# A hybrid mLSTM, HGRN and attention trunk: two-tile VectorE operations in scalar-tensor-tensor form, weight sums on VectorE outside HGRN, a recurrence whose two directions share their operations, and other places for some weight matmuls

## The chip, the cores and the metric

The kernel runs on one core of a Trainium2 chip. The metric is the device time of one execution in microseconds (us); what is compared is the median of several executions. TensorE is PE in the profile (its weight loads are PEld), VectorE is DVE, ScalarE is ACT, GpSimd is POOL and SyncE is SP. SP issues all the DMAs of the kernel. Within an engine, instructions run in the order of its queue: one that waits holds up all behind it.

## The reference

A trunk of two layers over 1024 tokens of width 1024, in fp32. Each layer normalises its input, multiplies it with one wide weight matrix, and feeds the columns of the product to three groups, whose outputs are gated, joined and projected back:

```python
proj = einsum("bsd,de->bse", rms_norm(x, norm_g[l]), w_in[l])
(xm, om, zm, hq, hff, hfb, hi, hz, aq, ak, av, az) = split(proj)
# mLSTM, 4 heads of 192, both directions, in chunks:
#   C, n are decayed and take in k v^T and k;  h = num / max(|den|, exp(-m_t))
hm  = sigmoid(om) * mlstm_bidirectional(mq, mk, mv, gates)
y_m = (head_rms_norm(hm) + m_skip[l] * xc) * silu(zm)      # xc = silu(conv(xm))
# HGRN, 6 heads of 128, both directions: S_t = diag(f_t) S_{t-1} + (1 - f_t) i_t^T, o_t = S_t^T q_t
f   = lb + (1 - lb) * sigmoid(hff or hfb)
y_h = head_rms_norm(hgrn2_bidirectional(hq, f_fwd, f_bwd, hi)) * silu(hz)
# differential attention, 4 heads: (softmax(Q1 K1^T) - lam softmax(Q2 K2^T)) V, partly rotated q and k
y_a = head_rms_norm(differential_attention(...)) * silu(az)
x   = x + einsum("bse,ed->bsd", concat(y_m, y_h, y_a), w_out[l])
```

## The kernel before

**The projection as a stream.** The product with `w_in` is cut into 32 units of four 512-wide weight quadrants each. The last 29 (`unit`, L197) are computed with seven products of 12 matmuls in place of eight, Strassen's way: a unit loads four quadrants (wraw), makes sums of them (ws, the four lines L213, L215, L229 and L236, on POOL), splits quadrants and sums into a rounded part (whi, ACT) and a rest (wlo, POOL), both L153 to L161, and adds the PSUM results to outputs c (DVE L221, L241, L247; ACT L252), which go to DRAM. `unit` is a generator that yields after every matmul and `fill(n)` (L467) draws n steps of it, so that weight matmuls (named ua, ub, ud) are strewn among the work of the stages as filler. `STEPS` is 84. The weight buffers are few: five of wraw, five each of whi and wlo, three of ws.

**The stages of a layer**, with their stretch of the span in us for the first layer (the second begins at 1590 and runs alike):

1. 0 to 294: norm, transposes, the first units, the convolution and gates of mLSTM. The convolution's last step is L612, its taps are L603 to L607.
2. 294 to 511: mLSTM (L733 to L829). First 420 steps of the stream, then four heads. In a head's recurrence, 8 chunks i for each of two directions d: products num and st on PE, n on ACT and DVE (L803, L804), the state C updated by two instructions (L815, L816: 128 and 64 rows of 193 columns), the denominator by three instructions of one column (L820 to L822), and n/den put or added into hsum (L825, L827). The two buffers of the tag m8 are shared by q (copied by ACT, L756) and hsum.
3. 511 to 972: HGRN, six heads in `hgrn(hd)` (L838 to L1019), a generator in three pieces, so that a head's end and the next head's start interleave. A head transposes v (hvt), turns the gate into ks and T (ACT L861, DVE L862 and L864), adds kd (L867), multiplies qp (L868, L869), multiplies kd with q (dg), then runs seven levels: each does matmuls lv between ks and qp and then multiplies both, in place, with decays T (DVE L938 and L939, one instruction over both directions) and halves T (L943). Then come kst, sb, sf, ho; squares of ho (ACT L1003, tile jk); `rstd` (L414 to L422, sums hss, tiles rs and hr); ho scaled (ACT L1009); its transposes (hyT), and the product hyo (L1017), which a DMA stores.
4. 972 to 1211: called md here. The rest of mLSTM: so is loaded (its DMA from pr_om), goes through ACT (L1069) and is transposed by PE (soT, L109), then gates hp (L1078); the convolution xcp is scaled on POOL (L1100); `rotate` turns the rotary columns (L1050 to L1052). 672 steps of the stream are placed behind marks, and then all that are left.
5. 1198 to 1482: attention (L1120 to L1215); 1277 to 1589: the output projection (op).

**What sets the order.** In mLSTM and HGRN `seq["on"]` is true, and every matmul and transpose is issued after the one before it in the program (`in_order`, L107): there the order on PE is that of the text, and the counts in `M_FILL` and `H_FILL` (L79, L80) say how many weight steps stand at each point. `H_FILL["tail"]` steps stand ahead of the first HGRN head of a layer. Elsewhere, and on all other engines everywhere, a list scheduler sets the order from estimated times. Buffers of the HGRN pool are shared by md's tiles and come free when the last head's instructions and its store are done.

Of the kernel before, what the change touches and what calls it, by code (L numbers as in the profile page):

```python
# [9 lines left out]
F32 = mybir.dt.float32  # L10
# [3 lines left out]
AF = mybir.ActivationFunctionType  # L14
# [65 lines left out]
H_FILL = {"hvt": 0, "ty": 32, "dg": 10, 0: 14, 1: 14, 2: 10, 3: 10, 4: 10, 5: 8, 6: 14, "kst": 10, "sb": 8, "ho": 10, "tail": 28}  # L80
# [15 lines left out]
def trunk(ctx, tc, x_in, positions, w_in, w_out, pvec, rvec, out, dbg=None):  # L96
# [20 lines left out]
    def tr(*a, **k):  # L117
        return in_order(nc.tensor.transpose, *a, **k)

# [47 lines left out]

    def w_tmp():
        cnt["n"] += 1
        return wp.tile([P, 512], F32, tag="ws", name=f"ws{cnt['n']}", bufs=3)  # L170
# [26 lines left out]
    def unit(l, u, B, dst):  # L197
# [15 lines left out]
        nc.gpsimd.tensor_tensor(s1, a21, a22, op=ALU.add)  # L213
        s2 = w_tmp()
        nc.gpsimd.tensor_tensor(s2, s1, a11, op=ALU.subtract)  # L215
# [13 lines left out]
        nc.gpsimd.tensor_tensor(s3, a11, a21, op=ALU.subtract)  # L229
# [6 lines left out]
        nc.gpsimd.tensor_tensor(s2, a12, s2, op=ALU.subtract)  # L236
# [169 lines left out]
    def rstd(ss, r, width):  # L406
# [12 lines left out]
        for _ in range(3):  # L419
            nc.vector.tensor_tensor(a, r, r, op=ALU.mult)  # L420
# [14 lines left out]
    for l in range(DEPTH):  # L435
# [50 lines left out]
        for half in range(2):  # L486
# [26 lines left out]
            else:  # L513
# [10 lines left out]
                for k in range(4):  # L524
# [9 lines left out]
                    tt = nc.vector.tensor_tensor  # L534
# [17 lines left out]
        if True:  # L552
# [47 lines left out]
            def post_xm(j, xm):  # L600
# [11 lines left out]
                nc.vector.tensor_mul(xc, xc, th)  # L612
# [37 lines left out]
        flr = m1.tile([P, 2, NT, 4], F32, name="flr")  # L650
        dec = m1.tile([P, 2, NT, 4], F32, name="dec")
        with tc.tile_pool(name=f"mb{l}", bufs=1) as mB:
# [27 lines left out]
            for d in range(2):  # L680
# [14 lines left out]
                nc.vector.tensor_sub(ir, ir, br)  # L695
# [27 lines left out]
            nc.vector.tensor_add(flr, b_tok, m_tok)  # L723
# [5 lines left out]
        with tc.tile_pool(name=f"mc{l}", bufs=1) as mp:  # L729
            for hd in range(MH):  # L730
# [60 lines left out]
                for i in range(NT):  # L791
                    for d in range(2):
# [5 lines left out]
                        n = mp.tile([P, MD + 1], F32, name=f"n{l}{hd}{d}{c}", tag="n", bufs=2)  # L798
# [8 lines left out]
                        if i < NT - 1:  # L807
# [3 lines left out]
                            pc2 = pc[r0:r0 + 64, 256:256 + MD + 1]  # L811
# [3 lines left out]
                            nc.vector.scalar_tensor_tensor(C[:, 0], C[:, 0], dc, pc[:, :MD + 1], op0=ALU.mult, op1=ALU.add)  # L815
                            nc.vector.scalar_tensor_tensor(C[r0:r0 + 64, 1], C[r0:r0 + 64, 1], dc[r0:r0 + 64], pc2,  # L816
                                                           op0=ALU.mult, op1=ALU.add)
                        fill(M_FILL[3])
                        den = mp.tile([P, 1], F32, name=f"den{l}{hd}{d}{c}", tag="den", bufs=4)
                        nc.vector.scalar_tensor_tensor(den, n[:, MD:], -1.0, n[:, MD:], op0=ALU.mult, op1=ALU.max)  # L820
                        nc.vector.tensor_tensor(den, den, flr[:, d, c, hd:hd + 1], op=ALU.max)
                        nc.vector.reciprocal(den, den)  # L822
                        if c not in seen:
                            seen.add(c)
                            nc.vector.tensor_scalar_mul(hsum[:, c], n[:, :MD], den)  # L825
                        else:
                            nc.vector.scalar_tensor_tensor(hsum[:, c], n[:, :MD], den, hsum[:, c], op0=ALU.mult, op1=ALU.add)  # L827
# [10 lines left out]
        def hgrn(hd):  # L838
# [19 lines left out]
            for d in range(2):  # L858
# [5 lines left out]
                nc.vector.tensor_scalar(th, th, lb_a1[:, l, d, hd:hd + 1], lb_a2[:, l, d, hd:hd + 1],  # L864
                                        op0=ALU.mult, op1=ALU.add)
            kd = slab(f"kd{hd}", "ha")
            nc.vector.tensor_tensor(kd, ks[:, 0], ks[:, 1], op=ALU.add)  # L867
            nc.vector.tensor_tensor(qp[:, 0], T0[:, 0], q, op=ALU.mult)  # L868
            nc.vector.tensor_tensor(qp[:, 1], T0[:, 1], q, op=ALU.mult)  # L869
# [18 lines left out]
            for lv in range(7):  # L888
# [44 lines left out]
                el = [[2 * hs, nb], [hs + S, 2], [1, hs]]  # L933
                tq = raw(T, 1, [[2, nb], [W - 1, 2], [0, hs]])
                tk = raw(T, W + 1, [[2, nb], [-W - 1, 2], [0, hs]])
                qv = raw(qp, 0, el)
# [410 lines left out]
```

## Time and profile before

| what | value |
| --- | --- |
| median of 3 runs | 3160.61 us (3159.49 to 3163.45) |
| the profiled execution's own time | 3164.39 us |
| its span | 3162.7 us |
| granted clock of PE, mean | 0.945 |
| busy: PE / DVE / ACT / POOL | 87% / 66% / 42% / 40% |

The profile is of one execution. A line of a group names the source line, the engine, the operation, out<-in by the program's names, the shapes, the count, then busy us and the mean ns of one, then the idle time of the engine ahead of them and what ended most of it. A line of waits names an engine's line, what it waited for, and us in total, times and the longest. A line of windows gives a stretch of the span, its length, the busy us (and instructions) of PE, PEld, DVE, ACT and POOL, PE's granted clock (1 is full), the DMA engines' busy share and GB/s. L109 is the matmul helper where the order is free, L111 where it is pinned.

### The profile page before, as it was taken

What the parts mean: (1) busy time and instruction counts of PE and PEld (TensorE: products, weight loads), DVE (VectorE), ACT (ScalarE), POOL (GpSimd) and SP (SyncE); (2) the same over time, 40 slices, a digit from 0 to 9 for tenths busy, and PEclk for the clock granted to TensorE, in tenths of its full rate; (3) what the DMA queues carried; (4) which work ended last, traced back from release to release, by engine and by line L of the source; (5) the groups of instructions that cost most, each with busy time, mean ns of one, the idle gap of its engine ahead of it and who ended that gap; (6) DMA issues with size and microseconds to landing.
All of it is one profiled execution on the core that took longest, in us unless ns stands there. A gap on an engine that the chain in (4) does not pass through costs nothing. (4 is left out here: it accounts for less than half of the span.)

```text
span 3162.7 us, 45081 instructions
## 1 busy us (share of the span) xinstructions
PE 2736.3 (87%) x16428; PEld 2242.7 (71%) x16428; DVE 2100.3 (66%) x3792; ACT 1320.4 (42%) x2732; POOL 1251.0 (40%) x881
## 2 busy tenths in 40 slices
PE   6888998888887998998979999978887889989987
PEld 4766877666665776887858787856666667768875
DVE  7775757777674526997587545767777644389964
ACT  5333443333433435654153344434433344365533
POOL 4255232454444771010243643234544457501012
PEclk9899999999998998999989999999999889989998
DMA  3333332222224654520223333232222256552221
GB/s 106 112 128 114 108 133 97 94 91 89 89 77 146 209 169 117 169 81 28 87 72 116 123 124 124 94 115 90 94 90 91 68 203 200 155 154 84 71 67 74
DMA packets 186526, 352.00 MB, mean 111 GB/s; under 512 B 17968, under 2 KB 67632, under 8 KB 186304
## 3 DMA queue, kind: packets, MB, share of 16 engines
q1 hardware_dynamic: 186304, 349.12, 33.4%
q8 instruction: 129, 2.11, 0.3%
q14 instruction: 93, 0.76, 0.1%
HBM read 234.69 MB, written 114.36 MB: 110 GB/s over the span
## 5 line engine op out<-in xcount | busy, mean ns | idle before, releaser
L161 POOL TENSOR_TENSOR wlo<-wraw,whi 128x512 fp32r<-128x512 f32 x262 | 404.7, 1554 | 1138.1 <-ACT whi L160 954.2
L161 POOL TENSOR_TENSOR wlo<-ws,whi 128x512 fp32r<-128x512 f32 x232 | 364.5, 1572 | 425.1 <-ACT whi L160 401.8
L109 PE MATMUL op<-whi,yb 128*128 128x512 f32 x1024 | 342.1, 402 | 1.5 <-DVE ayo L1163 0.7
L160 ACT ACTIVATE whi<-ws 128x512 fp32r<-128x512 f32 x232 | 145.8, 629 | 403.1 <-PE ua L109 161.3
L160 ACT ACTIVATE whi<-wraw 128x512 fp32r<-128x512 f32 x262 | 163.6, 627 | 313.5 <-issue 104.2
L109 PE MATMUL ua<-Bt,whi 128*128 128x512 f32 x698 | 231.4, 413 | 25.1 <-DVE c L241 24.2
L111 PE MATMUL ua<-Bt,whi 128*128 128x512 f32 x694 | 243.9, 424 | 4.6 <-DVE c L241 4.5
L1253 DVE TENSOR_TENSOR xo<-op,xo 128x512 f32<-128x512 f32 x256 | 173.9, 686 | 90.6 <-PE op L109 89.8
L109 PEld LDWEIGHTS op<-whi,yb 128*128 128x128 f32 x1024 | 193.9, 190 | 46.4 <-DVE xo L1253 1.8
L109 PE MATMUL op<-wlo,yb 128*128 128x512 f32 x512 | 203.0, 396 | 0.0
L1187 ACT ACTIVATE e<-S,mx 128x1024 f32<-128x1024 f32 x128 | 142.3, 1113 | 109.8 <-DVE mx L1184 45.3
L109 PEld LDWEIGHTS ua<-Bt,whi 128*128 128x128 f32 x698 | 135.2, 197 | 60.9 <-DVE c L241 27.0
L1183 DVE TENSOR_REDUCE mx<-S 128x1 f32<-128x1024 f32 x128 | 155.5, 1217 | 18.2 <-PE S L109 17.6
L111 PEld LDWEIGHTS ua<-Bt,whi 128*128 128x128 f32 x694 | 133.5, 196 | 35.1 <-DVE c L241 8.2
L109 PE MATMUL po<-av,wT 128*128 128x128 f32 x1024 | 139.8, 283 | 16.2 <-ACT wT L1203 9.7
L109 PEld LDWEIGHTS po<-av,wT 128*128 128x128 f32 x1024 | 131.4, 197 | 26.8 <-ACT wT L1203 13.1
L938 DVE TENSOR_TENSOR ks<-ks,T 128x1024 f32<-128x1024 f32 x84 | 141.5, 1684 | 11.0 <-ACT kt L894 10.5
L111 PE MATMUL ua<-Bt,wlo 128*128 128x512 f32 x348 | 147.4, 424 | 0.0
L939 DVE TENSOR_TENSOR qp<-qp,T 128x1024 f32<-128x1024 f32 x84 | 142.0, 1691 | 4.1 <-PE lv L111 4.1
L109 PE MATMUL ua<-Bt,wlo 128*128 128x512 f32 x348 | 141.8, 408 | 0.0
L109 PE MATMUL S<-qkh 128*128 128x512 f32 x256 | 111.9, 437 | 23.9 <-ACT e L1187 23.6
L894 ACT ACTIVATE kt<-ks 128x1024 f32<-128x1024 f32 x60 | 71.2, 1186 | 140.4 <-DVE ks L938 52.5
(437 smaller groups left out, 7011.9 us busy)
## 6 DMA issues: line engine op xcount, KB each, us to landing
wraw<-w_in SPq DMA_DIRECT2D x256, 256.0 KB
wraw<-yT SPq DMA_DIRECT2D x64, 256.0 KB
wraw<-w_out SPq DMA_DIRECT2D x64, 256.0 KB
xac<-xcd SPq DMA_DIRECT2D x16, 512.0 KB
W<-mu SPq DMA_DIRECT2D x32, 256.0 KB
xcd<-xc SPq DMA_DIRECT2D x12, 512.0 KB
xct<-tka SPq DMA_DIRECT2D x12, 512.0 KB
vd<-tkv SPq DMA_DIRECT2D x12, 512.0 KB
```

Of the source, the lines that this page charges most:

```text
L109: return fn(*a, **k)
L111: seq["last"] = fn(*a, **k)
L160: nc.scalar.activation(hi, src, AF.Copy)
L161: (lo_eng or nc.gpsimd).tensor_tensor(lo, src, hi.bitcast(F32), op=ALU.subtract)
L894: nc.scalar.activation(raw(kt, 0, [[2 * hs, nb], [hs, 2], [1, hs]]), raw(ks, 0, [[2 * hs, nb], [hs + S, 2], [1, hs]]), AF.Copy)
L938: nc.vector.tensor_tensor(kv, kv, tk, op=ALU.mult)
L939: nc.vector.tensor_tensor(qv, qv, tq, op=ALU.mult)
L1183: nc.vector.tensor_reduce(mx, ps, axis=AX.X, op=ALU.max)
L1187: nc.scalar.activation(e, ps, AF.Exp, scale=QK ** -0.5, bias=mx, accum_out=ls_)
L1253: nc.vector.tensor_tensor(xv, ps, xv, op=ALU.add)
```

## The change

Six edits, none of which changes what is computed:

1. `dtt(out, a, b, op)` issues (a * 1.0) op b as scalar_tensor_tensor, and takes the place of tensor_tensor for almost all DVE instructions with two SBUF tiles: in `rstd`, the convolution, HGRN (kd, qp, ks, T), rotate, attention's splits and the output projection's. In HGRN's levels, the instruction over both directions becomes one for each direction from level 1 on (128x512 each); level 0 stays one.
2. `wsum` puts the four weight sums of a unit on POOL while `sums["pool"]` is set, which it is from before the first HGRN head of a layer until after the last, and on DVE otherwise: 22 units of the 58 stay on POOL, 36 go to DVE, by the orders of the two kernels.
3. In the mLSTM recurrence the n of both directions lies in one tile nn. The three denominator instructions run once for both (two columns; flr is laid out for it), the C update is one instruction over both halves (386 columns), and the first hsum of a chunk is put by ACT; the second is added by DVE as before.
4. The second gate instruction of HGRN (L864) goes from DVE to ACT, as Identity with scale and bias.
5. The scaling of xcp (L1100) goes from POOL to ACT.
6. `H_FILL["tail"]` is 60 in place of 28, and 48 steps of the stream stand between the last HGRN head of a layer and md. md's own fixed counts stay, so 80 fewer steps are left for its end.

Where instructions move, in three places. First PE at the end of the first layer's HGRN stage: the last head's transposes (hyT), and md's first (soT). Before, no weight step lies between them:

```order
L111 MATMUL ud_22_8183<-Bt_0_350,whi_8159 128x512 x2
L111 MATMUL hyT_8193<-ident,ho_8121 128x128 x4
L111 MATMUL hyT_8199<-ident,ho_8121 128x128 x4
L109 MATMUL soT_8216<-ident,so_8213 128x128 x4
L109 MATMUL soT_8222<-ident,so_8213 128x128 x4
L109 MATMUL ud_22_8183<-Bt_0_350,wlo_8160 128x512
```

In the changed kernel the 48 steps begin and end so:

```order
L111 MATMUL hyT_8099<-ident,ho_8027 128x128 x4
L111 MATMUL hyT_8105<-ident,ho_8027 128x128 x4
L111 MATMUL ua_22_7794<-Bt_0_353,whi_8075 128x512
L111 MATMUL ua_22_7794<-Bt_0_353,wlo_8076 128x512
L111 MATMUL ua_22_7794<-Bt_0_353,whi_8075 128x512 x2
```

```order
L111 MATMUL ua_23_8139<-Bt_0_351,wlo_8159 128x512
L111 MATMUL ud_23_8202<-Bt_0_350,whi_8178 128x512 x2
L111 MATMUL ud_23_8202<-Bt_0_350,wlo_8179 128x512
L109 MATMUL soT_8216<-ident,so_8213 128x128 x4
L109 MATMUL soT_8222<-ident,so_8213 128x128 x4
```

The end of unit 22 and more than the first half of unit 23 now lie between hyT and soT. (At the start of HGRN it is alike: 32 more steps ahead of the first hvt.)

Second, DVE where the third HGRN head of the first layer begins and the second ends. Before (L862, L864 and kd, qp are the new head's; rs begins the old head's rstd):

```order
L862 TENSOR_SCALAR ks_5636<-T_02_5634,nlb_a_114,lb_a_112 128x1024 x2
L864 TENSOR_SCALAR T_02_5634<-T_02_5634,lb_a_112,lb_a_113 128x1024 x2
L867 TENSOR_TENSOR kd_5757<-ks_5636 128x1024
L869 TENSOR_TENSOR qp_5635<-T_02_5634,hq_5637 128x1024
L868 TENSOR_TENSOR qp_5635<-T_02_5634,hq_5637 128x1024
L416 TENSOR_SCALAR rs_5657<-hss_5567 128x8
```

In the changed kernel (L877 is L862 of before, L121 is `dtt`, L252 is L241, L427 is L416):

```order
L877 TENSOR_SCALAR ks_5504<-T_02_5502,nlb_a_114,lb_a_112 128x1024 x2
L121 SCALAR_TENSOR_TENSOR kd_5612<-ks_5504 128x1024
L121 SCALAR_TENSOR_TENSOR qp_5503<-T_02_5502,hq_5505 128x1024 x2
L252 TENSOR_TENSOR c_15_5574<-ua_15_5312,p_15_5555 128x512
L427 TENSOR_SCALAR rs_5525<-hss_5445 128x8
```

The two T instructions are gone from this queue, and an evacuation c of unit 15 has come to stand ahead of rs.

Third, DVE at the end of the first layer's HGRN stage. Before, the end of the last head's rstd, its two products hyo, and md's first hp:

```order
L421 SCALAR_TENSOR_TENSOR rs_8122<-rs_8122 128x8
L422 SCALAR_TENSOR_TENSOR hr_8064<-rs_8122,hr_8064 128x8
L1017 SCALAR_TENSOR_TENSOR hyo_8192<-hyT_8193,hgs,hz_8065 128x512
L1017 SCALAR_TENSOR_TENSOR hyo_8192<-hyT_8199,hgs,hz_8065 128x512
L1078 SCALAR_TENSOR_TENSOR hp_8210<-soT_8216,hp_8210 128x4x128
```

In the changed kernel (L432, L433 are L421, L422 of before, L1032 is L1017, L232 is L221, L1096 is L1078):

```order
L432 SCALAR_TENSOR_TENSOR rs_8028<-rs_8028 128x8
L433 SCALAR_TENSOR_TENSOR hr_7971<-rs_8028,hr_7971 128x8
L121 SCALAR_TENSOR_TENSOR ws_8469<-wraw_8442,wraw_8444 128x512
L1032 SCALAR_TENSOR_TENSOR hyo_8098<-hyT_8099,hgs,hz_7972 128x512
L1032 SCALAR_TENSOR_TENSOR hyo_8098<-hyT_8105,hgs,hz_7972 128x512
L121 SCALAR_TENSOR_TENSOR ws_8471<-ws_8469,wraw_8438 128x512
L121 SCALAR_TENSOR_TENSOR ws_8513<-wraw_8438,wraw_8442 128x512
L232 TENSOR_TENSOR c_23_8175<-ub_23_8162,p_23_8152 128x512
L1096 SCALAR_TENSOR_TENSOR hp_8210<-soT_8216,hp_8210 128x4x128
```

The three sums of unit 24 now stand in DVE's queue, the first ahead of hyo, and each waits there for its weight loads (wraw).

The diff, cut to its core (`-` before, `+` after):

```diff
-H_FILL = {"hvt": 0, "ty": 32, "dg": 10, 0: 14, 1: 14, 2: 10, 3: 10, 4: 10, 5: 8, 6: 14, "kst": 10, "sb": 8, "ho": 10, "tail": 28}
+H_FILL = {"hvt": 0, "ty": 32, "dg": 10, 0: 14, 1: 14, 2: 10, 3: 10, 4: 10, 5: 8, 6: 14, "kst": 10, "sb": 8, "ho": 10, "tail": 60}
...
+    def dtt(out_, a, b, op):
+        nc.vector.scalar_tensor_tensor(out_, a, 1.0, b, op0=ALU.mult, op1=op)
...
+    sums = {"pool": False}
+
+    def wsum(o, a, b, op):
+        if sums["pool"]:
+            nc.gpsimd.tensor_tensor(o, a, b, op=op)
+        else:
+            dtt(o, a, b, op)
...
-        nc.gpsimd.tensor_tensor(s1, a21, a22, op=ALU.add)
+        wsum(s1, a21, a22, ALU.add)
...
-                nc.vector.tensor_mul(xc, xc, th)
+                dtt(xc, xc, th, ALU.mult)
...
                 for i in range(NT):
+                    nn = mp.tile([P, 2, MD + 1], F32, name=f"n{l}{hd}{i}", tag="n", bufs=2)
                     for d in range(2):
...
-                        n = mp.tile([P, MD + 1], F32, name=f"n{l}{hd}{d}{c}", tag="n", bufs=2)
+                        n = nn[:, d]
...
-                            nc.vector.scalar_tensor_tensor(C[:, 0], C[:, 0], dc, pc[:, :MD + 1], op0=ALU.mult, op1=ALU.add)
-                            nc.vector.scalar_tensor_tensor(C[r0:r0 + 64, 1], C[r0:r0 + 64, 1], dc[r0:r0 + 64], pc2,
-                                                           op0=ALU.mult, op1=ALU.add)
+                            pc2 = pc.rearrange("p (b n) -> p b n", b=2)[:, :, :MD + 1]
+                            nc.vector.scalar_tensor_tensor(C, C, dc, pc2, op0=ALU.mult, op1=ALU.add)
                         fill(M_FILL[3])
...
-                        nc.vector.tensor_tensor(den, den, flr[:, d, c, hd:hd + 1], op=ALU.max)
+                    nc.vector.tensor_tensor(den, den, flr[:, i, hd], op=ALU.max)
...
-                            nc.vector.tensor_scalar_mul(hsum[:, c], n[:, :MD], den)
+                            nc.scalar.activation(hsum[:, c], nn[:, d, :MD], AF.Copy, scale=den[:, d:d + 1])
...
-                nc.vector.tensor_scalar(th, th, lb_a1[:, l, d, hd:hd + 1], lb_a2[:, l, d, hd:hd + 1],
-                                        op0=ALU.mult, op1=ALU.add)
+                nc.scalar.activation(th, th, AF.Identity, scale=lb_a1[:, l, d, hd:hd + 1], bias=lb_a2[:, l, d, hd:hd + 1])
...
-                nc.vector.tensor_tensor(kv, kv, tk, op=ALU.mult)
-                nc.vector.tensor_tensor(qv, qv, tq, op=ALU.mult)
+                for src, t_ in ((ks, (W + 1, 0)), (qp, (1, W))):
+                    if lv == 0:
+                        sv = raw(src, 0, [[2, nb], [1 + S, 2]])
+                        dtt(sv, sv, raw(T, t_[0], [[2, nb], [t_[1] - t_[0], 2]]), ALU.mult)
+                    else:
+                        for w in range(2):
+                            sv = raw(src, w * (hs + S), [[2 * hs, nb], [1, hs]])
+                            dtt(sv, sv, raw(T, t_[w], [[2, nb], [0, hs]]), ALU.mult)
...
+        sums["pool"] = True
         for hd in range(HH):
...
         next(prev)
+        sums["pool"] = False
+        fill(48)
         seq["on"] = False
...
-                    nc.gpsimd.tensor_scalar(xc, xc, mgs[:, l, 1, j:j + 1], None, op0=ALU.mult)
+                    nc.scalar.activation(xc, xc, AF.Copy, scale=mgs[:, l, 1, j:j + 1])
```

More of the change, by code (lines that the diff above doesn't have):

```diff
@@ L228, in unit @@
         s3 = w_tmp()
-        nc.gpsimd.tensor_tensor(s3, a11, a21, op=ALU.subtract)
+        wsum(s3, a11, a21, ALU.subtract)
         o5 = split(s3)
@@ L235, in unit @@
         nc.scalar.activation(p5, psd, AF.Copy)
-        nc.gpsimd.tensor_tensor(s2, a12, s2, op=ALU.subtract)
+        wsum(s2, a12, s2, ALU.subtract)
         o6 = split(s2)
@@ L649, in trunk @@
         wsv = m1.tile([P, 2, NT, 4], F32, name="wsv")
-        flr = m1.tile([P, 2, NT, 4], F32, name="flr")
+        flr = m1.tile([P, NT, 4, 2], F32, name="flr")
         dec = m1.tile([P, 2, NT, 4], F32, name="dec")
@@ L722, in trunk @@
                 nc.vector.tensor_sub(dec[:, d], mp_v[:, d, 0], mp_v[:, d, 1])
-            nc.vector.tensor_add(flr, b_tok, m_tok)
+            for d in range(2):
+                rv = (lambda a: a) if d == 0 else (lambda a: a[:, ::-1])
+                nc.vector.tensor_add(flr[:, :, :, d], rv(b_tok[:, d]), rv(m_tok[:, d]))
             for t in (ginter, wsv, dec):
@@ L814, in trunk @@
                             dc = dec[:, d, c, hd:hd + 1]
-                            nc.vector.scalar_tensor_tensor(C[:, 0], C[:, 0], dc, pc[:, :MD + 1], op0=ALU.mult, op1=ALU.add)
-                            nc.vector.scalar_tensor_tensor(C[r0:r0 + 64, 1], C[r0:r0 + 64, 1], dc[r0:r0 + 64], pc2,
-                                                           op0=ALU.mult, op1=ALU.add)
+                            pc2 = pc.rearrange("p (b n) -> p b n", b=2)[:, :, :MD + 1]
+                            nc.vector.scalar_tensor_tensor(C, C, dc, pc2, op0=ALU.mult, op1=ALU.add)
                         fill(M_FILL[3])
[L819 to L822, printed above, removed]
+                    den = mp.tile([P, 2], F32, name=f"den{l}{hd}{i}", tag="den", bufs=4)
+                    nc.vector.scalar_tensor_tensor(den, nn[:, :, MD], -1.0, nn[:, :, MD], op0=ALU.mult, op1=ALU.max)
+                    nc.vector.tensor_tensor(den, den, flr[:, i, hd], op=ALU.max)
+                    nc.vector.reciprocal(den, den)
+                    for d in range(2):
+                        c = i if d == 0 else NT - 1 - i
                         if c not in seen:
                             seen.add(c)
-                            nc.vector.tensor_scalar_mul(hsum[:, c], n[:, :MD], den)
+                            nc.scalar.activation(hsum[:, c], nn[:, d, :MD], AF.Copy, scale=den[:, d:d + 1])
                         else:
-                            nc.vector.scalar_tensor_tensor(hsum[:, c], n[:, :MD], den, hsum[:, c], op0=ALU.mult, op1=ALU.add)
+                            nc.vector.scalar_tensor_tensor(hsum[:, c], nn[:, d, :MD], den[:, d:d + 1], hsum[:, c],
+                                                           op0=ALU.mult, op1=ALU.add)
                 nc.sync.dma_start(hs_d[hd], hsum)
@@ L1049, in rotate @@
                 nc.sync.dma_start(s_, rope_d[1])
-                nc.vector.tensor_mul(w_, w_, s_)
-                nc.vector.tensor_mul(x_, x_, c_)
-                nc.vector.tensor_add(x_, x_, w_)
+                dtt(w_, w_, s_, ALU.mult)
+                dtt(x_, x_, c_, ALU.mult)
+                dtt(x_, x_, w_, ALU.add)
                 for g in range(4):
```

30 lines of the change are left out of this document (12 added, 18 removed).

## The prediction

> **What bounds the kernel now.** I read the page's first part, then TensorE's waits, then a table of windows by stage, then the groups by form for the instructions that the diff touches.
>
> ```profile
> span 3162.7 us, 45081 instructions
> PE 2736.3 (87%) x16428; PEld 2242.7 (71%) x16428; DVE 2100.3 (66%) x3792; ACT 1320.4 (42%) x2732; POOL 1251.0 (40%) x881
> ```
>
> PE is the busiest engine, 426 us idle. A change elsewhere counts only where PE waits for it. The waits of PE that the change can reach (line waited for: us in total, times, longest), and one of ACT behind the third:
>
> ```profile
> PE hyT L111 <- ACT ho L1009: 48.0, 12, 5.8
> PE lv L111 <- DVE qp L939: 46.2, 44, 2.6
> PE soT L109 <- ACT so L1069: 27.1, 2, 13.6
> PE q L111 <- ACT q L756: 16.4, 7, 2.7
> PE dg L111 <- DVE kd L867: 15.4, 2, 8.2
> PE hvt L111 <- DMA hvT<-pr_hi: 7.4, 2, 3.8
> ACT so L1069 <- DMA so<-pr_om: 28.8, 8, 12.8
> ```
>
> Three of them (dg, hvt, soT) occur once per layer, at the two seams of the HGRN stage: 22.8 us on entering it, 27.1 us on leaving it. The others recur in every head. By window (length, then busy us of PE, PEld, DVE, ACT, POOL, then PE's granted clock):
>
> ```profile
> 420.00:450.00 30.00, 29.98 (x171) 28.27 (x170) 26.75 (x99) 16.23 (x41) 6.61 (x13) 1.00 0.28 87
> 511.00:532.00 21.00, 10.21 (x57) 7.96 (x57) 10.60 (x10) 7.19 (x9) 5.27 (x4) 0.67 0.52 198
> 604.00:641.00 37.00, 31.40 (x347) 23.67 (x345) 36.29 (x32) 14.10 (x21) 23.93 (x12) 0.95 0.26 83
> 972.00:986.00 14.00, 0.47 (x3) 0.43 (x3) 0.75 (x1) 1.36 (x2) 0.00 (x0) 0.50 0.75 260
> 986.00:1211.00 225.00, 207.52 (x906) 167.34 (x905) 96.09 (x137) 87.11 (x182) 152.28 (x102) 0.95 0.55 180
> 1826.00:1855.00 29.00, 28.84 (x124) 22.93 (x123) 3.46 (x5) 12.98 (x28) 21.40 (x19) 1.00 0.33 113
> 2065.00:2085.00 20.00, 8.42 (x54) 7.12 (x55) 11.10 (x9) 7.26 (x9) 4.21 (x4) 0.74 0.54 197
> ```
>
> The mLSTM recurrence (420 to 450) is PE's: 29.98 of 30 us. HGRN's levels (604 to 641) are VectorE's: 36.29 of 37. The seams (511 to 532, 972 to 986, 2065 to 2085) are nobody's. What follows HGRN (986 to 1211) is 92% PE's. From 1826 to 1855 PE runs only matmuls of the projection: 124 in 29 us, 0.234 us for a weight step.
>
> **More weight steps at the seams.** Per layer 32 more steps run before HGRN's first head and 48 after its last one, and the PE-bound stage behind HGRN has 80 fewer. On entry, 64 x 0.234 = 15.0 us go into 22.8 us of idle. They replace waiting as long as the heads' loads come when they came before: these wait for buffers of mLSTM and not for PE. So -15.0, and 7.8 idle is left. The granted clock was 0.67 and 0.74 in these windows: busy times of 10.21 and 8.42 would be 6.8 and 6.2 at full clock, so up to -5.6; with most of the idle filled I take -4. Last, two instructions ahead of the first kd leave VectorE for ScalarE, L864, whose row beside that of the ScalarE instruction nearest to the new one is
>
> ```profile
> L864 DVE TENSOR_SCALAR T<-T,lb_a,lb_a 128x1024 f32<-128x1024 f32 x24 | 20.1, 873 | 0.1
> L861 ACT ACTIVATE T<-T 128x1024 f32<-128x1024 f32 x24 | 25.1, 1054 | 80.2 <-DMA T<-pr_ff 77.7 <-DMA T<-pr_fb 2.3
> ```
>
> so kd comes 2 x 0.873 sooner, -3.5 over the layers, taken as -3. Sum -22 (bounds: -24, and -8, if the extra weight loads push the heads' loads back by half of what the steps cover).
>
> On leaving, 96 x 0.234 = 22.5 us go into the 27.1 us for so. The so load is the last link; the weight loads of the new steps share the DMA engines with it, already 0.75 busy there, and VectorE has a weight sum ahead of the last hyo, whose store frees the buffers. I take 2 us per layer off: -18.5 (bounds -22.5, and 0, where the loads push so back by as much as the steps cover).
>
> **The mLSTM recurrence.** The groups, with count, busy us and mean ns:
>
> ```profile
> L816 DVE SCALAR_TENSOR_TENSOR C<-C,dec,st 64x193 f32<-64x193 f32 x112 | 46.1, 412 | 1.8
> L815 DVE SCALAR_TENSOR_TENSOR C<-C,dec,st 128x193 f32<-128x193 f32 x112 | 45.7, 408 | 1.2 <-PE st L111 1.0
> L821 DVE TENSOR_TENSOR den<-den,flr 128x1 f32<-128x1 f32 x128 | 29.9, 234 | 4.3
> L825 DVE TENSOR_SCALAR hsum<-n,den 128x192 f32<-128x192 f32 x64 | 28.2, 441 | 2.0
> L820 DVE SCALAR_TENSOR_TENSOR den<-n 128x1 f32<-128x1 f32 x128 | 25.9, 202 | 21.2 <-ACT n L806 19.0
> L822 DVE RECIPROCAL den<-den 128x1 f32<-128x1 f32 x128 | 20.8, 163 | 4.1
> ```
>
> Joining both directions halves the three den instructions: (29.9 + 25.9 + 20.8) / 2 = 38 us off VectorE. One C update of 386 columns replaces two of 193, 820 ns a pair. Between one column (202) and 193 (408) lie 206 ns, so 386 would take about 615, an estimate, and 112 x 0.205 = 23 us are saved; hsum's 28.2 us go to ScalarE, 16.23 of 30 us busy. Together some 89 us of VectorE, and the end does not move: PE is what these stretches wait for. I take 0. The bounds: -16.4, if the whole wait for q at the starts of heads came from late hsums; +6, if VectorE stalls at a weight sum there with the C update behind it.
>
> **HGRN's levels.** All that two-tile operations lose or gain by their form is read here:
>
> ```profile
> L939 DVE TENSOR_TENSOR qp<-qp,T 128x1024 f32<-128x1024 f32 x84 | 142.0, 1691 | 4.1 <-PE lv L111 4.1
> L938 DVE TENSOR_TENSOR ks<-ks,T 128x1024 f32<-128x1024 f32 x84 | 141.5, 1684 | 11.0 <-ACT kt L894 10.5 <-PE lv L111 0.5
> L867 DVE TENSOR_TENSOR kd<-ks 128x1024 f32<-128x1024 f32 x12 | 14.6, 1215 | 0.0
> L943 DVE TENSOR_TENSOR T<-T 128x1024 f32<-128x1024 f32 x12 | 17.2, 1435 | 26.3 <-PE dg L111 26.3
> L943 DVE TENSOR_TENSOR T<-T 128x512 f32<-128x512 f32 x12 | 9.0, 754 | 0.0
> L612 DVE TENSOR_TENSOR xc<-xc,xth 128x1024 f32<-128x1024 f32 x12 | 19.0, 1580 | 0.1
> L607 DVE SCALAR_TENSOR_TENSOR xc<-xm,pv,xc 128x1023 f32<-128x1023 f32 x24 | 39.0, 1630 | 0.3
> L1196 DVE SCALAR_TENSOR_TENSOR e<-e,cc,e 128x1024 f32<-128x1024 f32 x64 | 83.2, 1299 | 1.0
> L1253 DVE TENSOR_TENSOR xo<-op,xo 128x512 f32<-128x512 f32 x256 | 173.9, 686 | 90.6 <-PE op L109 89.8
> ```
>
> The same 1024 columns take 1215 ns at kd and 1690 in the levels, where POOL works beside them (23.93 of 37 us): about 470 ns are contention. The new form does not escape it: beside POOL, L607, already scalar-tensor-tensor, has a mean of 1630 and L612, tensor-tensor, 1580. The Trainium skill ("SBUF — State Buffer", Who interferes with whom) says that any VectorE instruction with two SBUF inputs contends with a GpSimd instruction that reads SBUF, whoever starts first; by it the form gains nothing, and these rows agree. Where POOL rests, L1196 takes 1299 against 1215, so the form alone adds 0 to 0.08 us to an instruction; I take 0.
>
> The split of ks and qp from level 1 on is a cost: 6 levels x 2 x 12 heads = 144 instructions become 288 of half the size. By L943's own two sizes a pair costs 2 x 0.754 - 1.435 = +0.073 us, in all +10.5; by L1253 and L867, 2 x 0.686 - 1.215 = +0.157, in all +23; at least 0, since no element goes away. VectorE sets the pace here, so I count it in full, by the nearer row: +10.
>
> **The head's turn in HGRN.** Behind PE's wait for ho stands this one:
>
> ```profile
> ACT ho L1009 <- DVE hr L422: 45.1, 12, 6.0
> ```
>
> hyT waits for ho, ho for hr, and hr's first instruction stands on VectorE behind the next head's ks, T, kd and qp. Without L864 it comes 2 x 0.873 = 1.75 us sooner; but qp, ahead of it, now waits for T from ScalarE, where two instructions of 1.054 stand among the squares of the head before. So -1.75 to +2.1 a head, -21 to +25 over twelve. ScalarE is free for much of it; I take -0.5 a head, -6.
>
> **Weight sums outside HGRN.** The sums of 36 of 58 units go to VectorE: 144 x 0.686 (L1253) = 99 us, spread over stages in which it has room (96.09 of 225 us behind HGRN). POOL, 152.28 of 225 there, loses more than that. The danger is in the wait that comes with them:
>
> ```profile
> L213 POOL TENSOR_TENSOR ws<-wraw,wraw 128x512 f32<-128x512 f32 x58 | 83.6, 1441 | 81.7 <-DMA wraw<-w_in 60.8 <-issue 14.7 <-PE soT L109 3.0
> POOL ws L213 <- DMA wraw<-w_in: 16.0, 6, 7.6
> POOL ws L213 <- DMA wraw<-w_in: 17.6, 6, 7.3
> PE ua L109 <- DVE c L241: 9.2, 2, 6.0
> ```
>
> (The second and third are the stage behind HGRN in each layer, the fourth is PE in the first of them.) On VectorE, evacuations c stand behind such a wait, and PE waits for c. Before, a c could also be held by work of its own queue, 9.2 us. The sums come about a unit, 84 steps, ahead of their use, so I take 0; bounds -9, and +60.8 if every wait reached PE. L1100's move to ScalarE relieves a POOL that is not waited for: 0.
>
> **Sum:** -22 - 18.5 + 10 - 6 = -36.5. The profiled execution's own time is 3164.4 (span 3162.7, 1.7 outside), 3.8 above the median of the runs, so it would become 3127.9; against the median of 3160.6 that is **3124**.
>
> **Rivals.** First, slower: sums on VectorE hold c and with it PE. For it speaks the wait row of 60.8 us over all units; against it, that PE had 84 steps of slack for most of these. If it all reached PE: -36.5 + 60.8 = +24, **3185**. It makes the kernel slower by over 6 us once 43 of the 60.8 reach PE. Chance 0.13.
>
> Second, the fills only move idle: the loads of the heads and of so come later by what the weight loads in front of them take. Then entry gives -8 and leaving 0, and with +10 - 6 the sum is -4: **3157**, within 0.2% (6.3 us) of before, which is about what a measurement of this kernel can tell from no change. For it speaks the DMA share of 0.75 at the seam. Chance 0.08.
>
> Third, the form does escape POOL: the levels' 168 instructions lose 470 ns each, -79 in all, **3045**. L607 against L612 speaks against it. Chance 0.05.
>
> Fourth, the form costs double: each instruction of the levels 1.2 us more, 168 x 1.2 = +202, **3326**. L1196's 1299 ns, with two inputs in SBUF, speaks against it. Chance 0.02. (The Trainium skill, "Vector Engine (DVE) Microarchitecture Reference", Points that are easy to get wrong, has such a rule: a scalar-tensor-tensor with two non-bf16 SBUF sources runs at half throughput. The trace does not bear it out.)
>
> **How the numbers follow.** The forecast has 0.72. Its own range: the terms lie 2, 4, 10, 15 and 16 us from their better bounds (entry, leaving, levels, turn, q) and 14, 18.5, 13 and 31 from their worse ones; squared, added and rooted that is 25 and 41: 3099 to 3165. The range of 8 in 10 leaves out the first, third and fourth rival, 0.20, and takes in the second. Its low end is nearly the sum of all better bounds (-24 - 22.5 - 21 - 16.4 = -84): 3080 to 3165. Within 0.2%: the second rival and the upper 0.05 of the forecast, 0.13. Faster by over 0.2%: the other 0.67 and the third rival, 0.72. Slower by over 0.2%: the first and the fourth, 0.15.
>
> **What would show it.** Right: the waits for hvt and kd at the entry fall from 22.8 us in all to some 5 to 8, the wait for so from 27.1 to under 9, the clock there rises; ks and qp at half size take over half of 1.69 us; PE stays saturated in the recurrence with VectorE some 40 us less busy per layer. Wrong: PE's waits for c grow past 40 us, hyT's 48.0 grow by more than 10, or a large scalar-tensor-tensor beside POOL comes near 1.2 us, or near 2.4 without POOL.

## The result, and the profile after

The changed kernel has a median of 3110.9 us against 3162.0 of the kernel before, a ratio of 0.9835 (95% interval 0.9807 to 0.9863): about 52 us, 1.65%, faster. 36.5 us were forecast. The profiled execution's span went from 3162.7 to 3108.1, 54.6 us.

The page's first two lines: PE did the same work in a shorter span, and POOL lost 266 us of busy time while VectorE, in spite of 144 weight sums more, has 43 us less.

```profile
span 3108.1 us, 44781 instructions
PE 2729.3 (88%) x16428; PEld 2243.4 (72%) x16428; DVE 2057.1 (66%) x3690; ACT 1374.4 (44%) x2832; POOL 984.5 (32%) x725
```

PE's waits, the rows that answer to those of before (us in total, times, longest):

```profile
PE lv L111 <- DVE qp L121: 67.7, 43, 4.5
PE hyT L111 <- ACT ho L1024: 48.9, 12, 5.7
PE q L111 <- ACT q L769: 14.5, 6, 2.4
PE dg L111 <- DVE kd L121: 5.7, 2, 3.0
PE soT L109 <- ACT so L1087: 4.8, 2, 2.5
```

The wait for hvt is gone, kd fell from 15.4 to 5.7 and so from 27.1 to 4.8. The wait in the levels rose from 46.2 to 67.7. The windows of the same stretches (recurrence, entry of the first layer, levels, leaving, the stage behind HGRN, entry of the second layer):

```profile
411.00:441.00 30.00, 30.00 (x166) 27.91 (x166) 17.02 (x50) 18.21 (x50) 6.70 (x13) 1.00 0.35 106
502.00:517.00 15.00, 12.05 (x78) 9.73 (x77) 8.40 (x7) 10.77 (x15) 8.95 (x7) 0.90 0.81 280
595.00:632.00 37.00, 29.47 (x335) 23.24 (x331) 33.37 (x44) 12.91 (x20) 24.63 (x11) 0.95 0.23 72
962.00:977.00 15.00, 12.52 (x51) 9.84 (x51) 2.83 (x4) 5.23 (x9) 5.13 (x4) 0.92 0.75 259
977.00:1166.00 189.00, 174.87 (x766) 140.73 (x765) 101.27 (x155) 81.44 (x169) 78.71 (x55) 0.95 0.59 194
2030.00:2050.00 20.00, 17.27 (x94) 13.88 (x95) 8.12 (x13) 9.51 (x14) 11.80 (x9) 1.00 0.77 258
```

In the recurrence VectorE fell from 26.75 to 17.02 of 30 us and PE stayed at 30. The seams, where PE was busy for 10.21 of 21 us and 0.47 of 14, now have 12.05 of 15 and 12.52 of 15, at a granted clock of 0.90 and above. POOL's busy time behind HGRN is 78.71 of 189 us, where it was 152.28 of 225.

Where the time went, stage by stage. The lengths are taken between the first or last matmuls of the names given, in the profiled executions; both layers are summed:

| stage, by PE's matmuls | before | after | difference |
| --- | --- | --- | --- |
| start to first q (norm, first units, convolution) | 521.5 | 511.9 | -9.6 |
| to last num (mLSTM) | 451.8 | 446.7 | -5.1 |
| to first dg (entry of HGRN) | 47.6 | 41.0 | -6.6 |
| to last hyT (six heads) | 886.9 | 892.9 | +6.0 |
| to first soT (leaving) | 27.8 | 29.9 | +2.1 |
| to last ua (md) | 450.6 | 401.2 | -49.4 |
| to last op (attention, output) | 754.8 | 763.1 | +8.3 |

The entry holds 64 more weight steps and the leaving 96 more; md holds 160 fewer. So the moved work shows in md. The border between the first two rows has moved as well: 19 more weight steps (4.4 us at 0.234 a step) run before the first q, and 19 fewer in mLSTM. A row of a single profile also moves without an edit in it: in the four profiles that have the heads as before (before, the fills alone, the fills with xcp, and those two with the sums), the six heads take 883 to 891 us.

### The profile page after: what moved, and what is told of

Same layout as the page of the kernel before. It is cut to its first block, busy times and chain, and to the rows that moved or that the text cites. A ratio compares the mean times of both kernels' runs of the same rounds, so it can differ in the third digit from the quotient of the medians.

```text
span 3108.1 us, 44781 instructions
## 1 busy us (share of the span) xinstructions
PE 2729.3 (88%) x16428; PEld 2243.4 (72%) x16428; DVE 2057.1 (66%) x3690; ACT 1374.4 (44%) x2832; POOL 984.5 (32%) x725
## 5 line engine op out<-in xcount | busy, mean ns | idle before, releaser
L164 POOL TENSOR_TENSOR wlo<-wraw,whi 128x512 fp32r<-128x512 f32 x262 | 390.3, 1496 | 1292.0 <-ACT whi L163 1152.5
L164 POOL TENSOR_TENSOR wlo<-ws,whi 128x512 fp32r<-128x512 f32 x232 | 347.3, 1498 | 581.2 <-ACT whi L163 510.9
L109 PE MATMUL ua<-Bt,whi 128*128 128x512 f32 x650 | 211.9, 406 | 13.7 <-ACT u L238 9.3
L121 DVE SCALAR_TENSOR_TENSOR qp<-qp,T 128x512 f32<-128x512 f32 (+1 forms) x156 | 166.9, 1106 | 3.6 <-PE lv L111 3.6
L121 DVE SCALAR_TENSOR_TENSOR ks<-ks,T 128x512 f32<-128x512 f32 (+1 forms) x156 | 151.6, 1001 | 23.1 <-ACT kt L908 13.8
L109 PE MATMUL po<-av,wT 128*128 128x128 f32 x1024 | 141.3, 285 | 20.4 <-ACT wT L1221 10.5
L109 PEld LDWEIGHTS ua<-Bt,whi 128*128 128x128 f32 x650 | 123.5, 193 | 44.4 <-ACT u L238 10.2
```

The source lines that it names most:

```text
L109: return fn(*a, **k)
L121: nc.vector.scalar_tensor_tensor(out_, a, 1.0, b, op0=ALU.mult, op1=op)
L164: (lo_eng or nc.gpsimd).tensor_tensor(lo, src, hi.bitcast(F32), op=ALU.subtract)
```

## The experiments

Each was timed beside the kernel before on its chip; a ratio of 0.0032 is 10 us. What was expected of a run draws on runs that were known by then, in part on some that stand further down.

**The fills alone.** The kernel before, with

```diff
-"ho": 10, "tail": 28}
+"ho": 10, "tail": 60}
...
         next(prev)
+        fill(48)
         seq["on"] = False
```

> The kernel before with one edit: 32 more weight steps ahead of the first HGRN head and 48 behind the last. Theory A (the filled seams carry the gain, the rest about cancels): the traces of before and of the changed kernel give, from the last recurrence matmul to the end of the md stage, 24.9 us less in the first layer and 28.9 in the second, and the edits beside the fills can reach only a few us of that; so 40 to 50 us faster than before. Rival B (the relief of VectorE and GpSimd carries the gain, the steps only move idle time): 0 to 20 us faster. Rival C (half and half: the fills give their 37.5 us of weight steps less what the loads take, and the sums on VectorE shorten the md stage beyond that): 30 to 38 us faster.

Measured 0.9895 (0.9873 to 0.9917), 33 us faster. That is theory C's number. The leaving went from 27.8 to 30.8 us, as in the changed kernel; the entry grew from 47.6 to 50.6 with its 64 more steps, where the changed kernel has 41.0; and md went only from 450.6 to 418.4, where the 160 steps are worth 37.4.

**Everything but the fills.** The changed kernel with `"tail": 28` and without `fill(48)`.

> The changed kernel without the moved weight steps, all other edits kept. Theory A: within 8 us of before. Rival B: 30 us or more faster than before. Rival C: 10 to 20 us faster than before. Where the effects add up, its gain and that of the fills alone together make the 51 us of the whole change.

Measured 1.0015 (1.0001 to 1.0029): nothing, 5 us slower if anything. Theory A's number for this one, so neither A nor C holds as a whole: 33 and -5 do not add up to 52. In its profile the first stages are 10 us shorter and the entries 5, the heads 18 longer (905.1), and md 3 longer (453.7). Some edit among the rest is worth time only once the fills are there.

**The sums back on GpSimd.** The changed kernel with

```diff
-    sums = {"pool": False}
+    sums = {"pool": True}
...
-        sums["pool"] = False
         fill(48)
```

> The changed kernel with all weight sums back on GpSimd. If the sums on VectorE are a gain beyond the forecast (the traces show the first stage of the first layer 8.5 us shorter and the end of md some 5 us a layer shorter than the moved steps explain), this is 10 to 20 us slower than the changed kernel. By the term of the forecast, 0, it is within 5 us of it. If the waits of VectorE for weight loads cost PE time, it is faster than the changed kernel.

Measured 0.9911 (0.9888 to 0.9934), some 24 us slower than the changed kernel; the profile says 21. Of these, 8.6 lie in the first stage of the layers (520.5 against 511.9), 5.4 in mLSTM, 7.7 in the heads, though the heads' own code is the same in both. The first stage with the sums on GpSimd holds 19 steps fewer and mLSTM 19 more, so nearly all of the 5.4 are steps, and the first stage differs by more than 8.6. In md, where I had looked for the danger, there is little: 403.9 against 401.2. The rival of the prediction, waits of VectorE for weight loads that hold up PE, did not come. VectorE does wait for the loads in the changed kernel, 40.1 us:

```profile
L121 DVE SCALAR_TENSOR_TENSOR ws<-wraw,wraw 128x512 f32<-128x512 f32 x72 | 54.1, 751 | 103.3 <-DMA wraw<-w_in 40.1 <-POOL wlo L164 33.8 <-issue 9.2
```

But PE's waits for c on VectorE, all rows of it added, are 27.7 us there, against 58.7 in the kernel before and 29.7 in this run. What the sums shorten is the first stage: in the first layer PE waits 13.8 us for c with them on GpSimd (9.1 and 4.7) and 7.3 with them on VectorE (4.0, 2.6 and 0.7).

**Joined levels.** The changed kernel with the level multiplies as before:

```diff
-                for src, t_ in ((ks, (W + 1, 0)), (qp, (1, W))):
...
+                nc.vector.tensor_tensor(kv, kv, tk, op=ALU.mult)
+                nc.vector.tensor_tensor(qv, qv, tq, op=ALU.mult)
```

> The changed kernel with HGRN's level multiplies of ks and qp as one instruction for both directions again, in the plain tensor-tensor form. Theory: the split costs VectorE time on the path; the trace gives 1.58 and 1.55 us for a joined ks and qp from level 1 on in the kernel before, and twice 0.885 and twice 0.991 for the pairs now, that is 0.19 and 0.43 us more for each of 72, some 45 us in all, of which the heads show only 6; so joined it is 10 to 30 us faster than the changed kernel. Rival: the shorter instructions let GpSimd in between and give the time back there, so within 5 us of it. The forecast's term says 10 us faster.

Measured 0.9742 (0.9719 to 0.9766), some 30 us faster than the changed kernel. The heads take 870.8 us in place of 892.9; 8 us more are gone from attention and the output, of which below. The groups, in the joined kernel and then in the changed one (count, busy us, mean ns):

```profile
L953 DVE TENSOR_TENSOR qp<-qp,T 128x1024 f32<-128x1024 f32 x84 | 142.4, 1695 | 1.5 <-PE lv L111 1.4
L952 DVE TENSOR_TENSOR ks<-ks,T 128x1024 f32<-128x1024 f32 x84 | 142.0, 1690 | 6.9 <-ACT kt L908 6.9
```

```profile
L121 DVE SCALAR_TENSOR_TENSOR qp<-qp,T 128x512 f32<-128x512 f32 x144 | 137.0, 991 | 3.6 <-PE lv L111 3.6
L121 DVE SCALAR_TENSOR_TENSOR ks<-ks,T 128x512 f32<-128x512 f32 x144 | 122.9, 885 | 9.3 <-PE lv L111 8.8
L121 DVE SCALAR_TENSOR_TENSOR qp<-qp,T 128x1024 f32<-128x1024 f32 x12 | 29.9, 2493 | 0.0
L121 DVE SCALAR_TENSOR_TENSOR ks<-ks,T 128x1024 f32<-128x1024 f32 x12 | 28.6, 2388 | 13.8 <-ACT kt L908 13.8
```

284 us of VectorE against 318 by these rows (the last two are level 0, which was never split): 34 us over 144 pairs, 0.24 us a pair. The single instructions in the two traces part this. With no work of GpSimd beside it, a pair takes 1.28 us from the first's start to the second's end (31 of the 144), and a joined instruction 1.21 (20 of the 144 from level 1 on). So the cut itself costs 0.07 us a pair, and the rest, some 0.17, arises only beside GpSimd.

**The split alone.** The kernel before, with the levels from 1 on split, in plain form.

> The kernel before with one edit: from level 1 on, ks and qp of HGRN are multiplied by one instruction for each direction (plain form). Theory (the split alone costs some 30 us in the changed kernel, which was 0.9 points faster with joined levels): 20 to 35 us slower than before. By the forecast's term 10 us slower. Rival (what joining gave is peculiar to the changed kernel's order): within 6 us of before.

Measured 1.0050 (1.0032 to 1.0068), 16 us slower; the heads are 21 us longer (908.0) in the profile, which is that of the longest of the six executions. Theory right in sign, its lower bound missed. The form is not what costs: these are tensor-tensor, and as long as the others.

```profile
L940 DVE TENSOR_TENSOR qp<-qp,T 128x512 f32<-128x512 f32 x144 | 136.3, 987 | 2.9 <-PE lv L111 2.9
L940 DVE TENSOR_TENSOR ks<-ks,T 128x512 f32<-128x512 f32 x144 | 127.6, 920 | 8.1 <-PE lv L111 7.9
```

**The plain form.** The changed kernel with

```diff
-        nc.vector.scalar_tensor_tensor(out_, a, 1.0, b, op0=ALU.mult, op1=op)
+        nc.vector.tensor_tensor(out_, a, b, op=op)
```

> The changed kernel with every two-tile operation of the helper in plain tensor-tensor form again, also the weight sums on VectorE; splits, places and counts are kept. Theory (the form is worth nothing): within 5 us of the changed kernel, and the half-size ks and qp keep means near 0.885 and 0.991 us. Rival 1 (the form escapes the contention with GpSimd): slower than the changed kernel by 20 us or more. Rival 2 (the form costs throughput): faster by 20 us or more.

Measured 0.9817 (0.9792 to 0.9843), the same as the changed kernel within the intervals. Its ks and qp:

```profile
L121 DVE TENSOR_TENSOR qp<-qp,T 128x512 f32<-128x512 f32 x144 | 136.2, 985 | 5.8 <-PE lv L111 5.8
L121 DVE TENSOR_TENSOR ks<-ks,T 128x512 f32<-128x512 f32 x144 | 128.4, 923 | 9.5 <-PE lv L111 9.2
```

Both rivals about the form fall.

**The gate back on VectorE.** The changed kernel with T's second instruction as L864 was.

> The changed kernel with the second gate instruction of HGRN (T) back on VectorE. By the forecast's term: 6 us slower, plus 3 us at the entry where kd comes later. Since the twelve heads of the changed kernel together are only 6 us longer than before while the split alone took some 30 us there (runs with joined levels), the other edits in the heads must give 16 us back; if that is the gate's move, this is 15 to 25 us slower than the changed kernel; if it is not, within 6 us.

Measured 0.9842 (0.9817 to 0.9867), no difference that this timing can tell. The profile has one: the heads are 905.1 us (892.9 in the changed kernel) and the entry 45.8 (41.0), 17 us in these stages, and 8 us less in attention and the output, of which below. The heads' 12 us alone prove little: they also took 898 to 905 us in four other runs that keep the split and the gate on ScalarE (without the fills 905.1, sums back 900.7, plain form 898.8, recurrence undone 898.2). Set beside each other, all profiles say more. With the gate on VectorE the heads take 905 and 908 us when the levels are split and 883 to 891 when they are joined; with the gate on ScalarE 893 to 905 when split and 868 to 877 when joined. The means differ by 7 and by 15 us, though other edits differ between these groups too. PE's waits with the gate back on VectorE:

```profile
PE hyT L111 <- ACT ho L1025: 51.1, 12, 5.5
PE dg L111 <- DVE kd L121: 10.5, 2, 5.3
```

**The fills, and xcp on ScalarE.** The fills alone, with

```diff
-                    nc.gpsimd.tensor_scalar(xc, xc, mgs[:, l, 1, j:j + 1], None, op0=ALU.mult)
+                    nc.scalar.activation(xc, xc, AF.Copy, scale=mgs[:, l, 1, j:j + 1])
```

> The kernel before with the moved weight steps and with the scaling of xcp on ScalarE. The fills alone gave 33 us, the whole change 52, the change without the fills nothing. Theory: the fills shorten the md stage to where GpSimd (135 of 196 us busy there, 12 scalings of 3 us among the splits) holds the transposes of mLSTM, which wait for their products; with that work gone, the md stage is some 7 us a layer shorter, so 10 to 16 us faster than with the fills alone, 43 to 50 us faster than before. Rival: the sums on VectorE are what the fills needed; then this is within 5 us of the fills alone.

Measured 0.9859 (0.9834 to 0.9883): 45 us, as the theory said. md falls from 418.4 to 407.5. PE's waits with the fills alone, and with both:

```profile
PE soT L109 <- ACT so L1070: 15.5, 4, 5.5
PE myT L109 <- issue: 13.7, 2, 6.9
PE myT L109 <- DVE hp L1091: 5.3, 6, 1.0
```

```profile
PE myT L109 <- DVE hp L1091: 6.9, 10, 1.0
PE soT L109 <- ACT so L1070: 4.9, 2, 2.5
```

And the windows behind HGRN in the first layer, fills alone and with xcp moved:

```profile
991.00:1187.00 196.00, 176.63 (x762) 141.68 (x760) 90.78 (x126) 75.71 (x163) 135.40 (x90) 0.93 0.57 185
```

```profile
989.00:1179.00 190.00, 177.12 (x766) 141.94 (x765) 85.55 (x126) 82.30 (x169) 112.91 (x84) 0.95 0.59 193
```

On GpSimd a scaling has a mean of 2988 ns, on ScalarE 1150. The waits that vanish are those of the second pair of mLSTM heads: 13.7 us for myT and 10.2 of the 15.5 for soT, against which others grow. These transposes do not read the scaled xcp; they read hp and so. The trace shows how the scaling reaches them. In the first layer (us of the span):

| step | fills alone | xcp on ScalarE too |
| --- | --- | --- |
| the first pair's last xcp is scaled | 1065.9 to 1068.7 | 1057.2 to 1058.4 |
| SP issues the store of that xcp | 1079.0 | 1062.6 |
| SP issues the last load of so, which stands behind it | 1087.5 | 1064.9 |
| ACT starts on this so | 1094.9 | 1070.5 |
| DVE does the second pair's rstd | 1110.0 to 1128.1 | 1086.8 to 1091.5 |
| PE starts on the second pair's myT | 1128.6 | 1093.0 |

So the scaling delayed a store, the store a load in the same queue, and that load all that follows. The scheduler's other orders have a part in it: with the fills alone a rotation that waits 7.5 us for a DMA stands ahead of this xcp on DVE, and with xcp moved it stands behind. What is the shorter scaling and what the new order was not told apart. The rstd lasts 18.1 us in one case, with the rotation's three instructions in between, and 4.7 in the other. Its instructions of 16 columns take 0.17 us where GpSimd is not in their way; in the first case most of them take 1.2 us, and six in a row end within 0.04 us of an instruction of GpSimd.

In the kernel before, VectorE waited 7.3 us for the scalings, but PE, with 80 more weight steps a layer to run, waited 2.9 us in all at myT. That is the gain which needed the fills. The scaling moved alone, in the kernel before, was not run.

**Those two and the sums.** The kernel before with the fills, xcp on ScalarE and `wsum` in plain form.

> The kernel before with three edits: the moved weight steps, the scaling of xcp on ScalarE, and the weight sums on VectorE outside HGRN (plain form). No split, no joined recurrence, no gate on ScalarE. Without the sums it was 45 us faster than before. Theory: the sums give what the first stage shows (7 us in the first layer, 1 in the second) and little else: 50 to 58 us faster than before. Rival 1: they give the 24 us that lay between the changed kernel with and without them: 65 to 72 us. Rival 2: their waits for weight loads cost: under 45 us.

Measured 0.9837 (0.9816 to 0.9858), 52 us faster: the whole gain of the changed kernel, with three of its six edits. The sums add 7 us to the two others. The first stage shows 4.9 of it (512.4 against 517.3 with the two, and 19 steps more), but that the two figures are near each other is chance: the other stages without attention give 16 more, of which some 7 are mLSTM at a lower granted clock in the profile without the sums (459.7 us at 0.976 and 0.986; with the fills alone it was 452.9 at 1.000, with the same matmuls), and attention and output take 17.1 back (765.8 against 748.7). The rest of the change (split, gate, recurrence, form) comes to nothing, as a sum.

**The recurrence undone.** The changed kernel with L798 to L827 as they were.

> The changed kernel with the mLSTM recurrence as before: three denominator instructions for each direction, two C updates, the first hsum on VectorE. Theory: PE sets the pace there, so the some 89 us of VectorE that come back cost nothing: within 5 us of the changed kernel. Rival (the 3.4 and 1.8 us by which the mLSTM stage became shorter, and the C update's place, are its work): 5 to 10 us slower.

Measured 0.9855 (0.9827 to 0.9882), 6 us slower at the middle, with intervals that overlap the changed kernel's. The mLSTM stage has 449.6 us against 446.7, with the same matmuls. PE is as saturated with VectorE's work back as without:

```profile
411.00:441.00 30.00, 30.00 (x168) 28.12 (x168) 25.50 (x92) 16.05 (x43) 6.69 (x13) 1.00 0.33 96
```

**More fills, joined.** The joined kernel with `"tail": 72` and `fill(58)`.

> The changed kernel with joined levels and 12 and 10 more weight steps at the two seams of each layer (72 and 58). The traces leave 5.7 us of waits for kd and 4.8 for so, over both layers; each layer moves 22 x 0.234 = 5.1 us of steps. Theory: what idle is left is filled, 2 to 8 us faster than with joined levels alone, 0.972 to 0.974 of before. Rival (the loads of the added steps push the seams' loads back, or the HGRN heads meet the stream at another place of its units): within 5 us or slower.

Measured 0.9743 (0.9721 to 0.9766), no better than joined alone. Rival, then: of the 10.3 us of steps, md lost 5.3 us, the entry and the leaving grew by 2.8, and the heads, 870.8 us in the joined kernel, took 877.1, which is no more than such a row moves by itself.

**Joined, and no sums on GpSimd at all.** The joined kernel without `sums["pool"] = True`.

> The changed kernel with joined levels, and with the weight sums on VectorE inside HGRN as well: 88 instructions more for VectorE there, of some 0.75 us, 66 us, and some 140 us less on GpSimd. Theory (VectorE sets the pace of the levels, and what it waits for of GpSimd's work goes with GpSimd's busy time): contention of the 168 level instructions, some 0.4 us each at 400 us of GpSimd in the heads, falls by a third, 22 us, against 66 more of which half lies beside other waits; so 5 to 30 us slower than with joined levels and sums on GpSimd. Rival (the heads have room for them, as the stages outside have): within 5 us or faster.

Measured 0.9722 (0.9704 to 0.9741), the fastest of all, though its interval overlaps the joined kernel's. The theory (5 to 30 us slower) falls. The level instructions got shorter:

```profile
L952 DVE TENSOR_TENSOR ks<-ks,T 128x1024 f32<-128x1024 f32 x84 | 130.1, 1549 | 15.3 <-ACT kt L908 15.3
L953 DVE TENSOR_TENSOR qp<-qp,T 128x1024 f32<-128x1024 f32 x84 | 140.7, 1675 | 0.3
```

by 14 us against the joined kernel's rows, less than the 66 that the sums were estimated to add, yet the heads did not get longer (868.3 against 870.8). The exception for HGRN in the change isn't needed.

## Why the prediction was right, and where its terms were off

Direction, place and order of size were right, and the range held the result. By its own steps:

- **Entry of HGRN**, forecast -22: the stretch is 6.6 us shorter and holds 15.0 us more work, -21.6. Right. Its parts were off and made up for each other: undoing the gate costs 4.8 there, where 3 was taken for kd, and the fills alone net -12 (47.6 to 50.6, with 15.0 of steps), where 19 was taken for steps and clock.
- **Leaving**, forecast -18.5: 2.1 longer with 22.5 more, -20.4. Right; the first soT comes a microsecond a layer later, where 2 were taken.
- **The stage behind HGRN.** The forecast credited the moved steps in full and L1100's move with 0, "a POOL that is not waited for". That is the step that failed. md fell by 49.4, 37.4 of it steps, 12 more. With the fills alone it fell by 32.2; with xcp on ScalarE as well by 43.1. In the run without the fills, where xcp is on ScalarE too, md is no shorter than before (453.7). So the time of GpSimd's scalings did not reach PE until the fills had taken their cover away. In the kernel before, a wait for it stood in the trace, of VectorE:

```profile
L1106 DVE SCALAR_TENSOR_TENSOR xcp<-myT,mgs,xcp 128x512 f32<-128x512 f32 x24 | 16.8, 740 | 7.3 <-POOL xcp L1100 7.3
```

The forecast had asked what hides each edit in the trace before and not in the kernel after the other edits.
- **The levels**, forecast +10: +21 in the heads and +16 in the time when done alone, -22 and -30 when undone. The sign was right, the size half, and the term left out what costs most. By L943's two sizes a pair costs 0.073 us more, which is what a pair without GpSimd beside it does cost (0.07), but this by luck: of L943's 12 long instructions, four ran beside GpSimd and made the mean 1435 ns, and the other eight have 1219. The prediction then counted nothing for GpSimd, though its own rows show it beside the levels. It adds the larger part of the 0.24 measured, more than the upper bound of 0.157. The 470 ns that the prediction put down to contention are too many as well: they hold level 0, which is long by itself (see the end). From level 1 on, ks and qp of the kernel before have means of 1577 and 1553 ns, against 1212 to 1215 with GpSimd at rest, some 350.
- **The head's turn**, forecast -6: by the groups of profiles above, -7 to -15. Size about right to twice too small. The wait that the term named holds only a part of it: with the gate back on VectorE, hyT waits 2.2 us longer for ho (51.1 against 48.9), and PE in the levels 5.8 longer for qp (73.5 against 67.7). The errors of this term and of the levels have opposite signs, so that the heads came out near the forecast (+4 against +6.0 measured) is luck.
- **Form of the two-tile operations**, forecast 0: right, by the plain form's run. As the Trainium skill says ("SBUF — State Buffer", Who interferes with whom), two SBUF inputs contend with GpSimd's reads in either form. The traces agree: half-size ks has 885 ns in one and 923 in the other, and with GpSimd at rest some 680 in both. The rule in "Vector Engine (DVE) Microarchitecture Reference" (Points that are easy to get wrong), half throughput for scalar-tensor-tensor on two non-bf16 SBUF sources, does not show: qp has 985 ns in plain form, 991 in the other. Level 0 in the new form, 2388 and 2493 ns, looks like the prediction's sign of a doubled cost, but it is as long in the kernel before, in plain form (2328 and 2517).
- **mLSTM**, forecast 0: -5.1 in the profile, of which 4.4 are the 19 steps that now run ahead of it; undoing the recurrence gives back 2.9. As argued, 89 us of VectorE bought next to nothing.
- **Weight sums**, forecast 0: -9.6 in the layers' first stage, which holds 19 steps more, where no term had looked. In time they are worth 7 us by the run of three edits and 24 by the run that undoes them in the changed kernel, which differ by more than their intervals. Without attention and the heads the profiles give 19 (some 7 of it the clock named above) and 17. What sets the two runs apart is mostly attention, 17.1 longer with the sums in the first pair of profiles and 4.5 in the second, and the heads, 2.4 and 7.7. The prediction's sign for its first rival, waits for c past 40 us, could not have told: by all rows they were 58.7 us in the kernel before. They fell to 29.2 with the fills alone and 27.7 in the changed kernel. Why c comes sooner in the first stage was not followed further.
- **Attention and output**: +8.3 in the changed kernel and no term. Part of it is PE's wait for ag (13.8 us, before 6.1). In the profiles of the joined kernel and of the one with the gate on VectorE the stage is back at 755, though none of its lines differ. The traces show what goes with it, the order that the list scheduler writes for PE's matmuls there. One order stands in both layers of four kernels (the changed one, plain form, recurrence undone, fills with xcp and sums): 379.4 to 384.6 us a layer. Another stands in both layers of four others (fills alone, fills with xcp, split alone, joined with no sums on GpSimd) and in the second of the joined kernel: 373.2 to 377.9. The remaining passes, in other orders, have 377.2 to 379.5. The mean granted clock is 0.97 in both groups, so it is not the clock; nor is it the new form there, since plain form has the slow order. No run changed this order alone. The stage differs by up to 17 us between two profiles (748.7 and 765.8), and a run that undoes one edit can be off by as much from what the edit itself does: undoing the gate costs 17 us in its stages and 2 in the time.

## What to carry to other kernels

When an edit removes a wait, ask again of every other edit whether its cover still stands: moving the scaling off GpSimd shortened md by 11 us once the fills were there, and md was no shorter in the run that had the move and not the fills. Moving filler into idle seams pays what the trace says, and the time shows in the stage from which the filler was taken. A split of an instruction on a saturated engine should be charged as it runs, beside the other engine's work, and not by a mean that mixes quiet and disturbed instructions. And where a scheduler may reorder a stage that no edit touches, that stage is to be taken out before two runs are compared.

## What was not expected of the hardware

Level 0's multiplies of ks and qp, with the same 1024 columns but directions and neighbours interleaved column by column, take 2.4 us (the two 128x1024 rows of the changed kernel), where the means over all levels are 1.7. In the kernel before, three of ks ran with GpSimd at rest, at 2.15 to 2.24 us, against 1.21 in later levels; the order of the columns is what differs between these. Identity with scale and bias from tiles on ScalarE takes 1257 ns on 1024 columns, where the prediction took the 1054 of its row for Tanh (1060 now, with a constant scale):

```profile
L879 ACT ACTIVATE T<-T,lb_a,lb_a 128x1024 f32<-128x1024 f32 x24 | 30.2, 1257 | 0.0
L876 ACT ACTIVATE T<-T 128x1024 f32<-128x1024 f32 x24 | 25.4, 1060 | 79.8 <-DMA T<-pr_ff 77.4 <-DMA T<-pr_fb 1.8
```

The C update of 386 columns took 611 ns, as estimated (615).

```profile
L829 DVE SCALAR_TENSOR_TENSOR C<-C,dec,st 128x386 f32<-128x386 f32 x112 | 68.4, 611 | 38.4 <-PE st L111 38.4
```
